# One address class for all tiles, and the conv's third input as seven quarter products: a hybrid decoder layer on one core

## The chip, the cores and the metric

The kernel runs on one core of one Trainium2 chip. The metric is the device time of one execution in microseconds: 962.82 us is the median of three runs of the kernel before (962.68 to 963.84). One more execution was profiled; it took 963.13 us, of which 961.4 us lie between its first and its last instruction (the span).

## What is computed

One decoder layer over 512 positions of 1,024 channels, in float32. Cut to its products and to what lies between them:

```python
h = rmsnorm(x, norm_mix_g)
proj = h @ w_in                      # 1024 x (9 * 1024 + 16)
bg, cg, xv, q, k, v, z, a, b, ga, gb = split(proj)
y_a = (bg * causal_dwconv(cg * xv, conv_a_w)) @ w_a_out      # 3 taps
y_b = gdn_branch(q, k, v, z, a, b, ...) @ w_b_out            # gated delta rule, chunks
mix = sigmoid(ga) * y_a + sigmoid(gb) * y_b
x = x + mix @ w_o
h = rmsnorm(x, norm_ffn_g)
up = causal_dwconv(h @ w_up, ffn_conv_w)                     # 1024 x 5632, 3 taps
x = x + (silu(up[gate]) * up[val]) @ w_down                  # 2816 x 1024
out = rmsnorm(x, norm_final_g)
```

`bg`, `cg` and `xv` are the three inputs of the short conv; `xv` is "the conv's third input" of the change.

## The kernel before, in words

**Products.** Each float32 matrix is held as the sum of a rounded part and a rest (`wh` and `wl` for weights, `x_[0]` and `x_[1]` for activations), and each product is made of three TensorE products: high by low, low by high, high by high. All go through `mm` (line 108), so the profile puts nearly all of TensorE's work on that one line.

**Jobs.** The kernel is a list of jobs that `run_jobs` takes in order. A job is a block of weights (1,024 x 256, 1 MB) and a use of it. While TensorE uses block i, ScalarE and VectorE split block i+1 into `wh` and `wl` tiles of 128 x 512 (`Block.part`, lines 137 to 141: a copy on ScalarE, then a subtraction on VectorE), and SP's queue loads block i+2. `wh` and `wl` have twelve slots each (`WQ`), so the split runs ahead of TensorE until it lacks a free slot. Small steps of work on the results (`evacs`), of the splits and of the delta rule's chain are put in between by `tick`, once for 2,048 columns of product.

**Two ways to use a block.** `col_job` makes two outputs of 128 x 512, each from 8 slices of the contraction with three products: 48 products of 512 columns in a job. A block is then split into 4 pairs of tiles. `sum_job` does the same 2 x 2 block product with 7 products of quarters in place of 8: its 7 weight tiles are sums and differences of the block's quarters (`SumBlock.split`, four extra VectorE operations at line 161), its activations are either quarters of the input or the sums held in `ts` (`us` in the second half), and its results are put together on VectorE and ScalarE (lines 292 to 309). It takes 84 products of 256 columns: 12 for each of 7 forms, in the order "11", "22", "s2", "s1", "s3", "s4", "12". "22", "s2", "s1" and "s3" take `ts`; the other three, 36 products, take the input itself.

**Where which is used.** The conv's groups 0 to 3 have three jobs each, `cg`, `xv`, `bg`. Group 0 is three `col_job`s. In groups 1 to 3 `cg` and `bg` are `sum_job`s; `xv` is a `col_job` in groups 1 and 2 and a `sum_job` in group 3 (lines 1141 to 1144). Then come three `sum_job`s and one `col_job` for `ga`, four `col_job`s each with `yas` and `yb` (`w_a_out`, `w_b_out`), the product with `w_o`, the 22 blocks of `w_up` (8 of them `sum_job`s) and the product with `w_down`. The products with `w_o` and `w_down` have the activations (`mix`, `mixb`, `xs`) as the stationary operand and the weights as the moving one; everywhere else the weights are stationary.

**What feeds VectorE in the conv's groups.** For a conv group the result of `cg` is held, `xv_c` multiplies by it (line 1121) and runs the conv's three taps (one ScalarE and two VectorE operations for each of two outputs, lines 335 and 338), and `bg_c` multiplies again (line 1130). All of this, the splits and the sums run on VectorE in the order in which they were issued.

**Where tiles lie.** A tile's address in its partition follows from the sizes of the tiles ahead of it, each rounded up to 32 bytes. In bytes, as the program before has them:

| tiles | address | modulo 256 |
|---|---|---|
| `wh`, 12 slots; `wl`, 12 slots | 19,232 + 2,048 n; 43,808 + 2,048 n | 32 |
| `hT`, `yb` (with its two halves in `hT`'s place), `h2` (`h` in the profile) | 68,384; 84,768; 101,152 | 32 |
| `ts`, `mix` (two tiles of 16,640 bytes) | 134,624; 151,264 | 224 |
| `yas` (in the same place, 32 elements further) | 134,752; 151,392 | 96 |
| `us`, `xs` | 151,520; 167,904 | 224 |
| `mixb` | 167,904 | 224 |

Slices of these tiles start at multiples of 512 or 1,024 bytes, so every operand of a product has its tile's remainder. The tiles from `ts` down the table are laid from the top end of the memory, those above from the bottom. A slot is taken over in the order in which slots come free, which is roughly, but not exactly, one after the other.

Of the kernel before, what the change touches and what calls it, by code (L numbers as in the profile page):

```python
# [9 lines left out]
F32 = mybir.dt.float32  # L10
# [6 lines left out]
P = 128  # L17
# [43 lines left out]
def layer_kernel(ctx, tc, x, norm_mix_g, w_in, w_ab, conv_a_w, gdn_conv_w, gdn_A_log, gdn_dt_bias,  # L61
# [60 lines left out]
            mm(o, ah, bh, False, i == n - 1, free)  # L122


    class Block:
        def __init__(self, src, quarter=(4, P)):
            self.src, self.quarter = src, quarter
            self.raw, self.ready, self.lead, self.fed = None, False, 2, True
            self.wh, self.wl = {}, {}

        def load(self):
# [3 lines left out]
            nc.sync.dma_start(out=self.raw, in_=self.src())  # L135

        def part(self, name, src):
            wh = self.wh[name] = wp.tile([P, *self.quarter], F32R, tag="wh", bufs=WQ, name=nm("wh"))
            wl = self.wl[name] = wp.tile([P, *self.quarter], F32R, tag="wl", bufs=WQ, name=nm("wl"))
            act.copy(out=wh, in_=src)  # L140
            dve.tensor_tensor(out=wl, in0=src, in1=wh.bitcast(F32), op=ALU.subtract)  # L141

# [8 lines left out]


    class SumBlock(Block):
        def split(self):
            if self.ready:
                return
            self.ready = True
            r = [self.raw[:, q] for q in range(4)]

            def to(q, a, b, op):  # L160
                dve.tensor_tensor(out=r[q], in0=a, in1=b, op=op)  # L161

            self.part("11", r[0])
            yield
            self.part("22", r[2])
            yield
            to(2, r[3], r[2], ALU.add)
            to(3, r[0], r[3], ALU.subtract)
            yield
            to(0, r[2], r[0], ALU.subtract)  # L170
            self.part("s2", r[0])
            yield
            self.part("s1", r[2])
            yield
            self.part("s3", r[3])
            yield
            to(0, r[1], r[0], ALU.subtract)
            self.part("s4", r[0])
            yield
            self.part("12", r[1])  # L180
            yield
# [34 lines left out]
            use(block.wh, block.wl)  # L216


    gate = const.tile([1, 16], F32, name="gate")

    def feed(raw):
        el = raw[0:1, 1].rearrange("p k n -> p (k n)") if len(raw.shape) == 4 else raw[0:1, 1]
# [204 lines left out]
    with tc.tile_pool(name="st1", bufs=1) as st1:  # L427
# [83 lines left out]
                                     op0=ALU.mult, op1=ALU.subtract)  # L511

        def round_k(q):
            wh = k_block.wh[q] = wp.tile([P, 4, P], F32R, tag="wh", bufs=WQ, name=nm("wh"))
            act.copy(out=wh, in_=k_block.raw[:, q])

        def rest_k(q):
            wl = k_block.wl[q] = wp.tile([P, 4, P], F32R, tag="wl", bufs=WQ, name=nm("wl"))
            dve.tensor_tensor(out=wl, in0=k_block.raw[:, q], in1=k_block.wh[q].bitcast(F32), op=ALU.subtract)


# [87 lines left out]
    Dms = {}  # L609

    def gates_chain(o):
        abT = gd.tile([P, S], F32, tag="cv", bufs=3, name="abT")[0:32]
        act.copy(out=abT, in_=o[0:32, :])
        yield
        o2 = bank()
        for n in range(NT):
            pe.transpose(out=o2[:, n * 32:(n + 1) * 32], in_=abT[:, n * P:(n + 1) * P], identity=ident[:32, :32])
        ab4 = o2[:, 0:128].rearrange("p (n c) -> p c n", c=32)
        abv = gd.tile([P, 16, NT], F32, name="abv")
        dve.tensor_copy(out=abv, in_=ab4[:, 16:32])  # L620
        dve.tensor_tensor(out=abv, in0=abv, in1=ab4[:, 0:16], op=ALU.add)
        T = lambda n: gd.tile([P, 32], F32, tag=n, name=nm(n))
        u, t, z, q, g = T("u"), T("t"), T("z"), T("q"), T("g")
        dve.tensor_tensor(out=hn(u), in0=abv[:, 0:8, :], in1=dtb.unsqueeze(2).broadcast_to([P, H, NT]), op=ALU.add)
        tc.keep_in_program_order(act.activation(out=hn(beta), in_=abv[:, 8:16, :], func=AF.Exp, scale=-1.0))
        tc.keep_in_program_order(act.activation(out=alg, in_=alg, func=AF.Exp))
        dve.tensor_scalar(t, u, -1.0, None, op0=ALU.mult)
        dve.tensor_tensor(out=t, in0=t, in1=u, op=ALU.min)
        tc.keep_in_program_order(act.activation(out=t, in_=t, func=AF.Exp))
        yield  # L630
        pool.tensor_scalar(beta, beta, 1.0, None, op0=ALU.add)
        pool.tensor_scalar(z, t, 2.0, None, op0=ALU.add)
        yield
        dve.reciprocal(out=beta, in_=beta)
        dve.reciprocal(out=z, in_=z)
        dve.tensor_scalar(u, u, 0.0, None, op0=ALU.max)
        yield
        pool.tensor_tensor(out=t, in0=t, in1=z, op=ALU.mult)
        pool.tensor_tensor(out=z, in0=t, in1=t, op=ALU.mult)
        pool.tensor_scalar(q, z, 1.0 / 15.0, 1.0 / 13.0, op0=ALU.mult, op1=ALU.add)  # L640
        for c in (11, 9, 7, 5, 3, 1):
            pool.tensor_tensor(out=q, in0=q, in1=z, op=ALU.mult)
            pool.tensor_scalar(q, q, 1.0 / c, None, op0=ALU.add)
        pool.tensor_tensor(out=q, in0=q, in1=t, op=ALU.mult)
        pool.tensor_scalar(q, q, 2.0, None, op0=ALU.mult)
        pool.tensor_tensor(out=g, in0=q, in1=u, op=ALU.add)
        pool.tensor_tensor(out=hn(g), in0=hn(g), in1=alg.unsqueeze(2).broadcast_to([P, H, NT]), op=ALU.mult)
        pool.tensor_scalar(g, g, -1.0, None, op0=ALU.mult)
        for _ in range(Y_G):
            yield  # L650
        o3 = bank()
        pe.matmul(o3[:, 0:32], lhsT=triu, rhs=g, start=True, stop=True)
        pe.matmul(o3[:, 32:64], lhsT=ones, rhs=g, start=True, stop=True)
        G, Gl = T("G"), T("Gl")
        dve.tensor_copy(out=G, in_=o3[:, 0:32])
        dve.tensor_copy(out=Gl, in_=o3[:, 32:64])
        dve.tensor_scalar(negG, G, -1.0, None, op0=ALU.mult)
        dve.tensor_tensor(out=kdv, in0=Gl, in1=G, op=ALU.subtract)
        act.activation(out=kdv, in_=kdv, func=AF.Exp)
        act.activation(out=eGl, in_=Gl, func=AF.Exp)  # L660
        act.activation(out=eG, in_=G, func=AF.Exp)
        dve.tensor_scalar(neG, eG, -1.0, None, op0=ALU.mult)
        yield
        o4 = bank()
        pe.transpose(out=o4[0:32, 0:P], in_=G, identity=ident)
        GT = gd.tile([32, P], F32, name="GT")
        dve.tensor_copy(out=GT, in_=o4[0:32, 0:P])
        nc.sync.dma_start(out=gtd, in_=GT)
        prep(0)
# [288 lines left out]
    def pair_jobs(pr):  # L958
        st = {}

        def qkv(which, j, o):
            c = gd.tile([P, S], F32, tag="cv", bufs=3, name=nm("cv"))
            yield from conv(c, o, gdn_w(which * 8 + 2 * pr + j), 4)
            if which == 1 and j == 0:
                reach(pr - 2, 99)
# [110 lines left out]
    def open_conv():  # L1076
        drain(evacs)
        drain(chains)
        drain(mids)
        drain(backs)  # L1080
        p2.close()
        sc = st["sc"] = p3.enter_context(tc.tile_pool(name="sc", bufs=1, side="right"))
        st["ts"] = [place(i, "ts").rearrange("p (m a n) -> p m a n", m=4, a=4) for i in range(2)]
        st["ya"] = sc.tile([P, ND, S], F32, name="ya")
        room["pool"] = sc
        adds.extend((Task(o_w.form()), Task(down_w.form())))
        sums_of.append(Task(activation_sums(hT, st["ts"], sc.tile([P, ND, S], F32, tag="mixa", name="xf"))))


    def place(i, name, up=0):  # L1090
        return st["sc"].tile([P, ND * S + 64], F32R, tag=f"t{i}", name=f"{name}{i}")[:, up:up + ND * S]

    def open_mix():
        st["mixa"] = st["sc"].tile([P, ND, S], F32, tag="mixa", name="mixa")
# [40 lines left out]
    for g in range(4):  # L1135
# [3 lines left out]
                     col_job(w_in, C_BG + g, hT, bg_c(g))]  # L1139
        else:  # L1140
            jobs += [sum_job(w_in, C_CG + g, hT, hsums, nothing, cg_place(g)),
                     sum_job(w_in, C_XV + g, hT, hsums, xv_c(g), pair_out) if g == 3 else
                     col_job(w_in, C_XV + g, hT, xv_c(g)),
                     sum_job(w_in, C_BG + g, hT, hsums, bg_c(g), pair_out)]

    def ga_c(g):
# [13 lines left out]
        return c  # L1160

    def split_ya():
        st["yas"] = [place(i, "yas", 32).rearrange("p (k n) -> p k n", k=ND) for i in range(2)]
        for k in range(ND):
            split(st["yas"], k, st["ya"][:, k, :])
            yield
# [24 lines left out]
    def wb_c(g):  # L1191
        def c(j, o):
            m = 2 * g + j
            t, mix = tmp("t"), st["mixa"][:, m, :]
            dve.tensor_tensor(out=t, in0=o, in1=sgb[0][:, m, :], op=ALU.mult)
            dve.tensor_tensor(out=mix, in0=t, in1=mix, op=ALU.add)
            yield
            if j == 1 and g % 2 == 1:
                if g == 1:
                    st["mix"] = [place(i, "mix").rearrange("p (m a n) -> p m a n", m=4, a=4) for i in range(2)]  # L1200
                yield from prep_a(mix_pairs(g - 1), st["mix"], g - 1)
        return c

# [248 lines left out]
    for g in range(NF // 2):  # L1452
# [6 lines left out]
        gj = up_job(g, gate_c(g), g < 2 or last, (lambda: splits.append(prep_d(prep_a, 0))) if last else None)  # L1459
        vj = up_job(NF // 2 + g, val_c(g), True)  # L1460
        gj[0].fed = vj[0].fed = g > 0
        jobs += [(gj[0], first_gate), (vj[0], first_val)] if g == 0 else [gj, vj]


# [216 lines left out]
```

## Time and profile before

| | us |
|---|---|
| median of three runs (lowest, highest) | 962.82 (962.68, 963.84) |
| profiled execution | 963.13 |
| its span | 961.4 |
| TensorE busy in the span | 950.7 (99%) |
| VectorE busy | 743.9 (77%) |
| ScalarE busy | 507.6 (53%) |
| GpSimd busy | 155.6 (16%) |

The granted TensorE clock is 0.998 of full speed. The page of the profile lists busy times by engine, the span in 40 slices, the chain that ended last, and groups of instructions. Products overlap in the records (each lasts longer than the distance to the next), so the time that a product costs is read from a stretch of the timeline divided by the number of products that start in it, and not from the mean duration. The count beside a stretch includes the records that reach into it from its edges.

### The profile page before, as it was taken

To read this page: it belongs to the slowest core of one execution; us is meant where nothing else is said; L and a number is where in the kernel's file an instruction comes from. 1 tells how busy PE (TensorE), PEld (TensorE's weight loads), DVE (VectorE), ACT (ScalarE), POOL (GpSimd) and SP (SyncE) were. 2 spreads that over 40 slices of the span, in tenths; PEclk is the share of its full clock that TensorE was granted. 3 is DMA by queue.
4 is the path that set the end of the run, shared out by engine and by line. 5 is a ranking of instruction groups with operands and counts; after the bars stand their busy time and mean duration, and the time that the engine had idled before them with its cause. 6 is when DMAs were issued, how large, how long until landed. Compare 5 with 4: busy or idle time off the path is not lost.

```text
span 961.4 us, 16188 instructions
## 1 busy us (share of the span) xinstructions
PE 950.7 (99%) x6188; PEld 823.1 (86%) x6188; DVE 743.9 (77%) x1401; ACT 507.6 (53%) x1073; POOL 155.6 (16%) x251
## 2 busy tenths in 40 slices
PE   8999999999999999999999999999999999999997
PEld 7888887987878889999988888998889999888885
DVE  6878686896725958799873479999988888969775
ACT  7895556565444434344651235645645456556463
POOL 3430300202000212312222100232222210000000
PEclk9999999999999999999999999999999999999999
DMA  6544312223121456667788435584775673176232
GB/s 227 157 137 123 94 53 89 75 57 93 53 89 45 144 130 140 175 162 170 215 270 174 120 112 217 152 231 162 177 191 180 185 160 132 45 264 228 100 132 88
DMA packets 51629, 138.11 MB, mean 144 GB/s; under 512 B 21691, under 2 KB 22112, under 8 KB 42848
## 3 DMA queue, kind: packets, MB, share of 16 engines
q1 hardware_dynamic: 38864, 107.45, 32.7%
q0 software_dynamic: 12544, 29.37, 16.1%
q8 instruction: 48, 0.79, 0.3%
q14 instruction: 29, 0.24, 0.1%
q10 hardware_dynamic: 144, 0.26, 0.1%
HBM read 133.64 MB, written 32.78 MB: 173 GB/s over the span
## 4 chain that ended last, share of the span: by engine, by line
PE 91%; DVE 4%; ACT 1%; issue 1%; POOL 1%; POOLq 0%
PE ps L108 83%; PE ps L689 1%; PE ps L724 1%; DVE wl L141 1%; PE ps L898 1%; PE ps L918 1%; DVE hn L1325 1%; DVE h L1339 1%; PE ps L907 1%; PE ps L886 0%; PE ps L885 0%; PE ps L862 0%; PE ps L856 0%; POOL r L1323 0%; PE ps L800 0%
## 5 line engine op out<-in xcount | busy, mean ns | idle before, releaser
L108 PE MATMUL ps<-hT,wh 128*128 128x512 f32 (+1 forms) x1104 | 318.1, 368 | 0.3 <-DVE hT L509 0.3
L140 ACT CAST wh<-raw 128x512 fp32r<-128x512 f32 x350 | 203.6, 619 | 217.0 <-PE ps L108 143.5
L141 DVE TENSOR_TENSOR wl<-raw,wh 128x512 fp32r<-128x512 f32 x350 | 233.3, 692 | 61.2 <-ACT wh L140 60.3
L108 PEld LDWEIGHTS ps<-hT,wh 128*128 128x128 f32 x1104 | 196.6, 189 | 28.9 <-DVE hT L509 0.5
L108 PE MATMUL ps<-hT,wl 128*128 128x512 f32 (+1 forms) x552 | 195.0, 361 | 0.0
L108 PE MATMUL ps<-h,wh 128*128 128x512 f32 (+1 forms) x704 | 177.7, 341 | 0.3 <-DVE h L1339 0.3
L108 PEld LDWEIGHTS ps<-h,wh 128*128 128x128 f32 x704 | 122.3, 189 | 15.6 <-DVE h L1339 0.5
L108 PEld LDWEIGHTS ps<-hT,wl 128*128 128x128 f32 x552 | 104.3, 189 | 13.8
L108 PE MATMUL ps<-h,wl 128*128 128x512 f32 (+1 forms) x352 | 114.5, 341 | 0.0
L108 PE MATMUL ps<-wh,xs 128*128 128x512 f32 (+1 forms) x320 | 96.9, 384 | 0.0
L108 PEld LDWEIGHTS ps<-h,wl 128*128 128x128 f32 x352 | 66.6, 189 | 7.6
L108 PEld LDWEIGHTS ps<-wh,xs 128*128 128x128 f32 x320 | 59.6, 188 | 13.1
L108 PE MATMUL ps<-wl,xs 128*128 128x512 f32 (+1 forms) x160 | 62.1, 388 | 0.0
L223 POOL COPY gate<-raw 1x1 f32<-1x1 f32 x38 | 16.7, 441 | 268.3 <-DMA raw<-in_w_in_dram 120.5
L338 DVE SCALAR_TENSOR_TENSOR cv<-ps,wA,cv 128x511 f32<-128x511 f32 (+2 forms) x72 | 53.2, 742 | 4.1 <-ACT cv L335 3.9
L108 PE MATMUL ps<-ts,wh 128*128 128x256 f32 x320 | 56.2, 276 | 0.0
L140 ACT CAST wh<-raws 128x512 fp32r<-128x512 f32 x66 | 39.3, 620 | 26.7 <-PE ps L108 8.9
L141 DVE TENSOR_TENSOR wl<-raws,wh 128x512 fp32r<-128x512 f32 x66 | 42.9, 687 | 12.5 <-ACT wh L140 12.5
L161 DVE TENSOR_TENSOR raw<-raw 128x512 f32<-128x512 f32 x72 | 49.5, 687 | 1.4
L108 PEld LDWEIGHTS ps<-ts,wh 128*128 128x128 f32 x320 | 49.0, 188 | 0.0
L108 PE MATMUL ps<-us,wh 128*128 128x256 f32 x256 | 45.0, 276 | 0.0
L108 PE MATMUL ps<-yas,wh 128*128 128x512 f32 x128 | 39.9, 391 | 0.0
(316 smaller groups left out, 1550.6 us busy)
## 6 DMA issues: line engine op xcount, KB each, us to landing
raw<-in_w_in_dram SPq DMA_DIRECT2D x35, 1024.0 KB, 5.3
raw<-in_w_up_dram SPq DMA_DIRECT2D x22, 1024.0 KB, 5.2
dv<-in_w_down_dram POOLq DMA_DIRECT2D x50, 256.0 KB, 6.1
raws<-dv SPq DMA_DIRECT2D x8, 768.0 KB, 5.8
ov<-in_w_o_dram POOLq DMA_DIRECT2D x20, 256.0 KB, 5.2
raws<-in_w_down_dram SPq DMA_DIRECT2D x10, 512.0 KB, 6.0
raw<-in_w_a_out_dram SPq DMA_DIRECT2D x4, 1024.0 KB
raw<-in_w_b_out_dram SPq DMA_DIRECT2D x4, 1024.0 KB, 6.6
```

The source lines that it names most:

```text
L108: pe.matmul(o, lhsT=a, rhs=b, start=start, stop=stop, skip_group_check=free)
L140: act.copy(out=wh, in_=src)
L141: dve.tensor_tensor(out=wl, in0=src, in1=wh.bitcast(F32), op=ALU.subtract)
L161: dve.tensor_tensor(out=r[q], in0=a, in1=b, op=op)
L223: tc.keep_in_program_order(pool.tensor_copy(out=gate[:, 0:1], in_=el[:, 0:1]))
L338: dve.scalar_tensor_tensor(out=dst[:, sh:], in0=src[:, :S - sh], scalar=wcol(j), in1=dst[:, sh:], op0=ALU.mult, op1=ALU.add)
L689: pe.transpose(out=o[:, n * P:(n + 1) * P], in_=src[:, n * P:(n + 1) * P], identity=ident)
L724: pe.matmul(o[:, i], lhsT=kqs[:, a, h, 0, sl], rhs=kqs[:, b, h, :, sl], start=a > 0, stop=a + b == 0)
L898: pe.matmul(o[:, 0:P], lhsT=TTf[:, f, :], rhs=rs[h], start=True, stop=True)
L907: pe.matmul(o2[:, 0:P], lhsT=kn[:, f, :], rhs=vns[h], start=True, stop=True)
L918: pe.matmul(o[:, 0:P], lhsT=A[:, f, :], rhs=vns[h], start=True, stop=True)
L1325: dve.scalar_tensor_tensor(out=hn_[:, sl], in0=x1[:, t, sl], scalar=r, in1=st["gff"][:, sl], op0=ALU.mult, op1=ALU.mult)
```

## The change

The diff has two parts.

*Layout.* `gate` grows from 16 to 64 elements (64 to 256 bytes). Each `wh` and `wl` slot grows from 512 to 528 elements, and a tile starts either at the slot's beginning or 16 elements (64 bytes) further: the blocks of `sum_job`, the first block (`k_block`) and the first two blocks of `w_up` start 64 bytes in, the others at the beginning. `place` goes: `ts`, `yas` and `mix` become plain tiles of 16,384 bytes, and `yas` is no longer moved by 128 bytes. To make room, the tiles `cv` have two buffers in place of three, and `wb_c` takes its temporary from the tag `c`, which `xv_c` used before, in place of a tag `t` of its own.

*Third input.* `xv` of groups 1 and 2 becomes a `sum_job`, as that of group 3 is.

```diff
+    UP = 16
+    def slot(tag, up, *dims):
+        t = wp.tile([P, 4 * P + UP], F32R, tag=tag, bufs=WQ, name=nm(tag))[:, up:up + 4 * P]
+        return t.rearrange("p (a b) -> p a b", a=dims[0]) if len(dims) == 2 else t
...
-            wh = self.wh[name] = wp.tile([P, *self.quarter], F32R, tag="wh", bufs=WQ, name=nm("wh"))
-            wl = self.wl[name] = wp.tile([P, *self.quarter], F32R, tag="wl", bufs=WQ, name=nm("wl"))
+            wh = self.wh[name] = slot("wh", self.up, *self.quarter)
+            wl = self.wl[name] = slot("wl", self.up, *self.quarter)
...
     class SumBlock(Block):
+        def __init__(self, src):
+            super().__init__(src)
+            self.up = UP
...
-    gate = const.tile([1, 16], F32, name="gate")
+    gate = const.tile([1, 64], F32, name="gate")
...
-            wh = k_block.wh[q] = wp.tile([P, 4, P], F32R, tag="wh", bufs=WQ, name=nm("wh"))
+            wh = k_block.wh[q] = slot("wh", UP, 4, P)
...
-        abT = gd.tile([P, S], F32, tag="cv", bufs=3, name="abT")[0:32]
+        abT = gd.tile([P, S], F32, tag="cv", bufs=2, name="abT")[0:32]
...
-            c = gd.tile([P, S], F32, tag="cv", bufs=3, name=nm("cv"))
+            c = gd.tile([P, S], F32, tag="cv", bufs=2, name=nm("cv"))
...
-        st["ts"] = [place(i, "ts").rearrange("p (m a n) -> p m a n", m=4, a=4) for i in range(2)]
+        st["ts"] = [sc.tile([P, 4, 4, HS], F32R, tag=f"t{i}", name=f"ts{i}") for i in range(2)]
...
-    def place(i, name, up=0):
-        return st["sc"].tile([P, ND * S + 64], F32R, tag=f"t{i}", name=f"{name}{i}")[:, up:up + ND * S]
...
-                     sum_job(w_in, C_XV + g, hT, hsums, xv_c(g), pair_out) if g == 3 else
-                     col_job(w_in, C_XV + g, hT, xv_c(g)),
+                     sum_job(w_in, C_XV + g, hT, hsums, xv_c(g), pair_out),
...
-        st["yas"] = [place(i, "yas", 32).rearrange("p (k n) -> p k n", k=ND) for i in range(2)]
+        st["yas"] = [st["sc"].tile([P, ND, S], F32R, tag=f"t{i}", name=f"yas{i}") for i in range(2)]
...
-            t, mix = tmp("t"), st["mixa"][:, m, :]
+            t, mix = tmp("c"), st["mixa"][:, m, :]
...
+        if g == 0:
+            gj[0].up = vj[0].up = UP
```

More of the change, by code (lines that the diff above doesn't have):

```diff
@@ L127, in __init__ @@
             self.src, self.quarter = src, quarter
-            self.raw, self.ready, self.lead, self.fed = None, False, 2, True
+            self.raw, self.ready, self.lead, self.fed, self.up = None, False, 2, True, 0
             self.wh, self.wl = {}, {}
@@ L513, in round_k @@
         def round_k(q):
-            wh = k_block.wh[q] = wp.tile([P, 4, P], F32R, tag="wh", bufs=WQ, name=nm("wh"))
+            wh = k_block.wh[q] = slot("wh", UP, 4, P)
             act.copy(out=wh, in_=k_block.raw[:, q])
         def rest_k(q):
-            wl = k_block.wl[q] = wp.tile([P, 4, P], F32R, tag="wl", bufs=WQ, name=nm("wl"))
+            wl = k_block.wl[q] = slot("wl", UP, 4, P)
             dve.tensor_tensor(out=wl, in0=k_block.raw[:, q], in1=k_block.wh[q].bitcast(F32), op=ALU.subtract)
@@ L1199, in c @@
                 if g == 1:
-                    st["mix"] = [place(i, "mix").rearrange("p (m a n) -> p m a n", m=4, a=4) for i in range(2)]
+                    st["mix"] = [st["sc"].tile([P, 4, 4, HS], F32R, tag=f"t{i}", name=f"mix{i}") for i in range(2)]
                 yield from prep_a(mix_pairs(g - 1), st["mix"], g - 1)
```

## The prediction

> **What bounds the kernel now.** I read the page first: its busy times, the granted clock and the chain of waits.
>
> ```profile
> span 961.4 us, 16188 instructions
> PE 950.7 (99%) x6188; PEld 823.1 (86%) x6188; DVE 743.9 (77%) x1401; ACT 507.6 (53%) x1073; POOL 155.6 (16%) x251
> PEclk9999999999999999999999999999999999999999
> PE 91%; DVE 4%; ACT 1%; issue 1%; POOL 1%; POOLq 0%
> ```
>
> TensorE has no idle time to win and its clock never drops. The kernel gets shorter only by fewer columns of product or by products that run closer together. So the second view is the groups by shape, for the counts (a row with `wl` and half the count belongs to each of these, and `mixb` adds 24 and 12):
>
> ```profile
> L108 PE MATMUL ps<-hT,wh 128*128 128x512 f32 x800 | 260.4, 400 | 0.0
> L108 PE MATMUL ps<-h,wh 128*128 128x512 f32 x384 | 119.8, 389 | 0.0
> L108 PE MATMUL ps<-wh,xs 128*128 128x512 f32 x304 | 94.0, 390 | 0.0
> L108 PE MATMUL ps<-h,wh 128*128 128x256 f32 x320 | 60.7, 284 | 0.3 <-DVE h L1339 0.3
> L108 PE MATMUL ps<-hT,wh 128*128 128x256 f32 x304 | 58.9, 284 | 0.3 <-DVE hT L509 0.3
> L108 PE MATMUL ps<-ts,wh 128*128 128x256 f32 x320 | 56.2, 276 | 0.0
> L108 PE MATMUL ps<-us,wh 128*128 128x256 f32 x256 | 45.0, 276 | 0.0
> L108 PE MATMUL ps<-yas,wh 128*128 128x512 f32 x128 | 39.9, 391 | 0.0
> L108 PE MATMUL ps<-yb,wh 128*128 128x512 f32 x128 | 39.6, 389 | 0.0
> L108 PE MATMUL ps<-wh,mix 128*128 128x512 f32 x88 | 27.8, 391 | 0.0
> ```
>
> The third view is stretches of the timeline, cut at the first product of each kind: 48 products with `ts`; 36 of 256 columns with `hT`; the `xv` job of group 1 (48 of 512), then its first 6 products alone; `yas` (192); `yb` (191); two `h` jobs (96); all with `xs` (456 of 512 columns, 24 of 256).
>
> ```profile
> core 0: us, PE busy (x), PEclk, DMA share, GB/s
> 386.43:391.89 5.46, 5.46 (x50) 1.00 0.99 269
> 382.13:386.43 4.30, 4.30 (x38) 1.00 0.81 271
> 364.33:375.24 10.91, 10.91 (x51) 1.00 0.77 168
> 364.33:365.72 1.39, 1.39 (x9) 1.00 0.76 93
> 484.88:528.84 43.96, 43.96 (x193) 1.00 0.81 210
> 528.84:572.18 43.34, 43.34 (x192) 1.00 0.40 116
> 638.10:659.89 21.79, 21.79 (x98) 1.00 0.49 122
> 846.70:954.00 107.30, 107.07 (x479) 1.00 0.48 166
> 951.50:954.15 2.65, 2.65 (x24) 1.00 0.11 41
> ```
>
> Divided, products of one shape differ with their tiles. 256 columns: 113.7 ns with `ts`, 119.4 with `hT`. 512 columns: 226.9 with `yb`, 227.0 with `h`, 229.0 with `yas`. The tail's 256-column products with `xs` stand about 117.8 apart (22.5 in 2.65 us), which leaves (107.30 - 24 x 0.118) / 456 = 229.1 for its 512-column ones. No engine is waited for in these stretches; what differs is where the tiles lie. With D for the stationary operand's remainder modulo 256 less the moving one's, the table of addresses gives: D = 0 (`hT`, `h`, `yb`) 119.4 and 226.9; D = 64 (`ts`, `us`) 113.7; D = 192 (`yas`, `xs`, `mix`) 117.8 and 229.0. No row shows D = 128, and none D = 64 at 512 columns.
>
> So most of the work already stands at the better end of what these rows show for 512 columns: 1,968 of 2,784 products at 226.9 to 227.3, 816 (`yas`, `xs`, `mix`, `mixb`) at 229. At 256 columns 864 stand at 113.7 and 936 at 119.4.
>
> The Trainium skill (SBUF — State Buffer, section "A bandwidth-pool intuition that's wrong (but worth ruling out)") gives TensorE two independent read ports, one for the moving operand and one for weight loads. By that rule D would not matter and the layout would be worth nothing; the 113.7 beside 119.4 ns for one shape speaks against it, but it stays a rival below.
>
> **Where the change puts tiles.** `gate` moves everything from the bottom by 192 bytes, and the 24 longer slots add 24 x 64 = 1,536, which is 6 x 256. So `hT`, `h2` and `yb` go from 32 to 224, the remainder that the tiles from the top have; `yas` goes from 96 to 224. All activations are then alike. The weights are not: a slot is 528 x 4 = 2,112 bytes, 8 x 256 + 64, and the first starts at 19,424, remainder 224. Slot n has remainder 224 + 64 n: the twelve slots go round 224, 32, 96, 160, three times. The 64 bytes of `up` turn this ring by one place and leave it a ring. A block's four or seven tiles take slots nearly in order, so each block meets all four D, and D changes from tile to tile; before, it was one value through a whole stage.
>
> **The sum, part by part.**
>
> *Third input.* Two jobs of 48 products (10.91 us) become jobs of 84: 48 at 113.7 and 36 at 119.4, which is 5.46 + 4.30 = 9.76. That is -1.15 each, **-2.3**.
>
> *256 columns.* Now (864 x 113.7 + 936 x 119.4) / 1,800 = 116.7 ns. Spread over four D: 119.4, 113.7, 117.8 and an unknown, for which I take their mean, so 117.0. On 1,800 products and the 168 new ones **+0.6**. Bounds: all at 113.7, -5.4 us; all at 119.4, +5.0.
>
> *512 columns.* 2,688 are left: 1,872 at about 227 and 816 at 229.0. With D = 0 for a quarter and the one row of unlike remainders (229.0) for the rest, the mean is 228.5: 1,872 x 1.5 = +2.8, 816 x -0.5 = -0.4. Then there is settling: the first 6 products of the `xv` job take 231 ns, 26 ns above pace together, before they fall into step. With a tile change every 2 to 6 products there are some 750 changes of D. I charge each a tenth of that settling, because only the address changes and not the length: +1.9. Together **+4.4**. Bounds: all at 226.9, -1.7; each product 5.7 ns above that, as D = 0 is above D = 64 at 256 columns, +13.6.
>
> *VectorE's new work.* Rows of before, for the stage of groups 1 and 2 and for group 3 with `ga`, then one sum job's operations:
>
> ```profile
> core 0: us, PE busy (x) PEld busy (x) DVE busy (x) ACT busy (x) POOL busy (x), PEclk, DMA share, GB/s
> 354.60:414.00 59.40, 59.40 (x422) 55.61 (x421) 48.67 (x81) 24.66 (x46) 12.72 (x20) 1.00 0.71 167
> 414.00:473.97 59.97, 59.97 (x518) 59.97 (x517) 52.67 (x91) 28.58 (x57) 12.49 (x22) 1.00 0.63 182
> ACT wh L140 <- PE ps L108: 15.6, 7, 4.3
> 413.82 0.68 DVE L297 TENSOR_TENSOR v<-ps,u 128x512 f32<-128x512 f32 x1
> 414.42 0.68 DVE L161 TENSOR_TENSOR raw<-raw 128x512 f32<-128x512 f32 x1
> 415.02 0.68 DVE L303 TENSOR_TENSOR o<-ps,v 128x512 f32<-128x512 f32 x1
> 415.62 0.41 DVE L305 TENSOR_TENSOR o<-ps,v 128x256 f32<-128x256 f32 x1
> 417.75 1.89 DVE L141 TENSOR_TENSOR wl<-raw,wh 128x512 fp32r<-128x512 f32 x3
> 466.90 2.49 DVE L141 TENSOR_TENSOR wl<-raw,wh 128x512 fp32r<-128x512 f32 x4
> ```
>
> Long operations follow each other 0.60 us apart, half ones 0.33. A sum job in place of a column job adds 3 `wl`, 4 of line 161, lines 297 and 303 and the halves of 293 and 305: 9 x 0.60 + 2 x 0.33 = 6.1 us, 12.1 for two, while TensorE's time for them shrinks by 2.3. So VectorE has 14.4 us less room. Cover: 10.7 idle in the first stretch, where ScalarE's copies wait 15.6 us for TensorE to free slots (this line of the waits belongs to that stretch alone), and the lead at the end: the last four `wl` are done from 467.5 on for a job that starts at 473.97, about 6.5. 17.2 covers 14.4 if at most 2.8 of it cannot be reached. In the second stretch VectorE left 7.3 idle though its lead was shrinking, so some idle time is a wait for ScalarE and stays. I take **+0.7**, with bounds 0 and 14.4 - 6.5 = 7.9 (none of the idle reached). Past that point `wl` of `bg` in group 3 and of the `ga` jobs is late, and TensorE waits for it. ScalarE gets 3 copies and 2 halves more for each job and is at 24.66 of 59.4; the blocks' loads and the POOL queue's DMAs for each job stay as they are.
>
> *Nothing:* `cv` with two buffers, because the third conv's first write and the Silu that empties its buffer stand in order on ScalarE (without that order, one conv's length, some 3 us, once); `c` for `t`, because no conv is left then.
>
> Sum: -2.3 + 0.6 + 4.4 + 0.7 = +3.4, on the profiled execution's 963.1 gives 966.5; the median lies 0.3 under that execution: **966.2**. Its own range is 963 to 971.
>
> **Rivals.**
> - *The slots' ring costs nothing.* The unlike D average out, or matter only over whole stages, and the third input alone counts: 962.8 - 2.3 = 960.5. For it: all observed differences are 1 to 5%. Against: 229.0 in 192 products in a row.
> - *The layout does what its words say,* every pair at the best row: 816 x -2.1 ns = -1.7, 936 x -5.7 = -5.3, and two jobs of 84 x 113.7 in place of 10.91 us = -2.7; with +1.5 for VectorE, about 954.6. Against it: the arithmetic of 2,112 bytes.
> - *VectorE becomes the bound* (slower side): its lead is used up in group 2, and from `xv` of group 3 to the last `ga` TensorE waits for `wl`. It decides when more than 2.8 us of the idle time can't be reached; at 6 us, with the layout as forecast, 971.5.
> - *D = 64 and D = 128 are bad at 512 columns,* 5.7 ns above: half of 2,688 x 5.7 = +7.7 in place of the 2.8 or so that they have in the sum: about 971 to 975.
>
> **How the numbers follow.** Forecast 0.45; the ring costs nothing 0.22; as its words say 0.10; VectorE 0.13; bad D 0.10. A difference under 0.2%, 1.9 us, can't be told from none here. Faster: 0.10 + 0.17 of the second = 0.27; the same: 0.05 of it and 0.10 of the forecast's lower end, 0.15; slower 0.58. The range 957 to 973 leaves out the layout as its words say and the upper part of the last two.
>
> **What would show it.** In the same stretches: `hT` and `yb` at 512 columns at 228 to 230 in place of 227, and no longer even from tile to tile; 256 columns near 117 for both kinds; the first six `sum_job`s of the conv at 9.8 us each; a wait of TensorE for `wl` of line 141 between 430 and 475 under 2 us. The forecast is wrong if 512-column products stand at 227 or less throughout, or if TensorE waits there for more than 3 us.

## The result, and the profile after

The changed kernel takes 974.12 us (median of 4 runs, 973.51 to 974.60) beside 963.33 us (962.68 to 964.52) for the kernel before on the same chip: ratio 1.011, 95% interval 1.0093 to 1.0128. The direction was forecast, the size was not: +10.8 us in place of +3.4, outside the range. The profiled execution took 973.51 us.

The page of the kernel after, its span, busy times, granted clock and the chain by engine:

```profile
span 971.8 us, 16362 instructions
PE 958.5 (99%) x6260; PEld 825.8 (85%) x6260; DVE 757.0 (78%) x1423; ACT 510.6 (53%) x1083; POOL 153.6 (16%) x251
PEclk9999999999999999999999999999999999999999
PE 81%; DVE 12%; ACT 2%; issue 2%; POOL 1%; POOLq 0%; ACTq 0%; DVEq 0%
```

The span grew by 10.4 us, the clock did not change, and TensorE is still busy for 99% of it: it is busy for 7.8 us longer. The chain shows something new too. VectorE's share of it went from 4% to 12%, at TensorE's cost.

Stretches of TensorE's timeline of the kernel after, each cut at the first product of its kind and of the next (length, TensorE busy with the number of records, granted clock, DMA share, GB/s). In order: 180 products of 512 columns with `hT`; 48 of 256 with `ts`; 36 of 256 with `hT`; `yas` (192); `yb` (192); two `h` jobs (96); then twice the 36 products of 256 columns with `hT` between two `ts` parts, later in the conv's groups:

```profile
315.41:357.12 41.71, 41.71 (x183) 1.00 0.43 124
358.49:364.09 5.60, 5.60 (x51) 1.00 0.40 88
364.09:368.36 4.27, 4.27 (x39) 1.00 0.38 159
489.10:533.59 44.49, 44.49 (x194) 1.00 0.88 233
533.59:578.03 44.44, 44.44 (x193) 1.00 0.39 113
643.77:666.00 22.23, 22.23 (x98) 1.00 0.49 121
413.15:418.21 5.06, 4.48 (x39) 1.00 0.38 43
443.37:449.38 6.01, 4.48 (x39) 1.00 0.75 222
```

At 512 columns that is 231.7, 231.7, 231.5 and 231.6 ns a product. The kernel before had 229.0 with `yas` and 226.9 to 227.2 with the others (the prediction shows its rows but for the same 180 products with `hT`):

```profile
313.68:354.58 40.90, 40.90 (x184) 1.00 0.43 125
```

All these stages now run at nearly one pace, and it is worse than the worst of before. At 256 columns the job shown has 116.7 with `ts` and 118.6 with `hT`, against 113.7 and 119.4. The last two rows have idle time inside a TensorE stretch, 0.6 and 1.5 us, which no such stretch had before.

Single products with `yb` of the kernel after (start, duration, line, operation, tiles):

```profile
545.14 0.40 PE L108 MATMUL ps<-yb,wh 128*128 128x512 f32 x1
545.38 0.39 PE L108 MATMUL ps<-yb,wl 128*128 128x512 f32 x1
545.61 0.39 PE L108 MATMUL ps<-yb,wh 128*128 128x512 f32 x1
545.83 0.39 PE L108 MATMUL ps<-yb,wl 128*128 128x512 f32 x1
546.07 0.39 PE L108 MATMUL ps<-yb,wh 128*128 128x512 f32 x1
546.29 0.40 PE L108 MATMUL ps<-yb,wl 128*128 128x512 f32 x1
546.53 0.40 PE L108 MATMUL ps<-yb,wh 128*128 128x512 f32 x1
```

In the kernel before, the products with `yb` stand evenly:

```profile
545.44 0.39 PE L108 MATMUL ps<-yb,wl 128*128 128x512 f32 x1
545.66 0.39 PE L108 MATMUL ps<-yb,wh 128*128 128x512 f32 x1
545.89 0.39 PE L108 MATMUL ps<-yb,wl 128*128 128x512 f32 x1
546.12 0.39 PE L108 MATMUL ps<-yb,wh 128*128 128x512 f32 x1
```

In the trace's nanoseconds these are 226 or 227 apart. In the kernel after, the distances from 545.14 on are 235, 229, 229, 231, 226, 236, 235. The stationary tile's slot changes at each of them, and D, worked out from the addresses that the program gives its tiles, goes 0, 128, 192, 64, 192, 64, 0.

VectorE in the conv's groups of the kernel after (busy time of PE, PEld, DVE, ACT and POOL), and what TensorE waited for (total, times, longest):

```profile
356.00:416.00 60.00, 59.42 (x504) 59.01 (x503) 54.43 (x92) 25.11 (x50) 12.58 (x20) 1.00 0.60 148
416.00:476.00 60.00, 58.47 (x500) 58.31 (x500) 56.74 (x98) 31.62 (x64) 12.93 (x22) 1.00 0.66 164
436.00:446.00 10.00, 9.88 (x86) 9.68 (x84) 9.97 (x17) 5.19 (x10) 2.85 (x4) 1.00 0.62 124
```

```profile
PE ps L108 <- DVE u L305: 2.3, 3, 1.5
```

TensorE is idle for 0.6 and 1.5 us in these two stretches of 60 us; in the like stretches of before it was busy throughout. Around a wait VectorE has nothing left: it is busy for 9.97 of the 10 us from 436 on.

Where the 10.4 us are, by stage, from the starts of the same products in both traces: 2.5 up to the first `ts` job, 1.7 in the conv's groups 1 to 3 and `ga`, 1.4 in `yas` and `yb`, 0.3 in the product with `w_o`, 4.5 from the first product with `h` to the end. By kind, summed over the distance from each product's start to the next (a distance over 1.2 times the usual pace of its kind counts at that pace, and the rest of it as a gap), for the two kernels and for two experiments told below:

| us | before | after | layout alone | third input alone |
|---|---|---|---|---|
| products of 512 columns: number, mean ns, sum | 2,784, 228.1, 635.1 | 2,688, 231.4, 622.0 | 2,784, 231.3, 644.0 | 2,688, 228.2, 613.3 |
| products of 256 columns | 1,951, 116.7, 227.8 | 2,119, 117.1, 248.2 | 1,951, 117.3, 228.9 | 2,119, 116.7, 247.3 |
| gaps | 13.7 | 17.0 | 13.9 | 19.3 |
| span | 961.4 | 971.8 | 972.4 | 964.7 |

So the change is, in products alone and at the paces of before, (2,119 - 1,951) x 116.7 ns - 96 x 228.1 ns = -2.3 us; the pace at 512 columns adds 622.0 - 613.3 = 8.7; that at 256 columns 0.9; the gaps 3.3. Together 10.6, against 10.4 of span. (The count at 256 columns includes the delta rule's own products, which the change doesn't touch.)

### The profile page after: what moved, and what is told of

It reads as the page before. It is cut to its first block, busy times and chain, and to the rows that moved or that the text cites. A ratio compares the mean times of both kernels' runs of the same rounds, so it can differ in the third digit from the quotient of the medians.

```text
span 971.8 us, 16362 instructions
## 1 busy us (share of the span) xinstructions
PE 958.5 (99%) x6260; PEld 825.8 (85%) x6260; DVE 757.0 (78%) x1423; ACT 510.6 (53%) x1083; POOL 153.6 (16%) x251
## 4 chain that ended last, share of the span: by engine, by line
PE 81%; DVE 12%; ACT 2%; issue 2%; POOL 1%; POOLq 0%; ACTq 0%; DVEq 0%
PE ps L108 74%; DVE wl L149 4%; DVE raw L173 2%; PE ps L701 1%; PE ps L736 1%; ACT wh L148 1%; DVE c L350 1%; PE ps L910 1%; PE ps L930 1%; DVE o L315 1%; DVE h L1346 0%; PE ps L919 0%; DVE hn L1332 0%; PE ps L898 0%; PE ps L897 0%
## 5 line engine op out<-in xcount | busy, mean ns | idle before, releaser
L108 PE MATMUL ps<-hT,wh 128*128 128x512 f32 (+1 forms) x1088 | 308.7, 364 | 2.6 <-DVE u L305 2.3
L149 DVE TENSOR_TENSOR wl<-raw,wh 128x512 fp32r<-128x512 f32 x356 | 236.3, 688 | 66.0 <-ACT wh L148 64.3
L108 PEld LDWEIGHTS ps<-hT,wh 128*128 128x128 f32 x1088 | 191.6, 188 | 31.2 <-issue 1.7
L108 PE MATMUL ps<-hT,wl 128*128 128x512 f32 (+1 forms) x544 | 188.8, 357 | 0.0
L108 PE MATMUL ps<-ts,wh 128*128 128x256 f32 x384 | 69.2, 279 | 0.0
L108 PEld LDWEIGHTS ps<-ts,wh 128*128 128x128 f32 x384 | 59.5, 189 | 0.0
L173 DVE TENSOR_TENSOR raw<-raw 128x512 f32<-128x512 f32 x80 | 54.9, 686 | 1.1
L108 PE MATMUL ps<-ts,wl 128*128 128x256 f32 x192 | 47.0, 279 | 0.0
```

What stands on the lines that cost most here:

```text
L108: pe.matmul(o, lhsT=a, rhs=b, start=start, stop=stop, skip_group_check=free)
```

## The experiments

Three theories stood at the start. Theory 1: D, the stationary tile's remainder modulo 256 less the moving one's, sets the distance of products, and the ring of 2,112-byte slots puts half of them at bad values and leaves them unsettled. Theory 2: the extra `sum_job`s make VectorE the bound, and that is the main loss. Theory 3: the alikeness of the tiles is itself bad, wherever they lie. Each kernel below computes the whole layer.

### The two parts alone

The layout without the third input:

```diff
-                     sum_job(w_in, C_XV + g, hT, hsums, xv_c(g), pair_out),
+                     sum_job(w_in, C_XV + g, hT, hsums, xv_c(g), pair_out) if g == 3 else
+                     col_job(w_in, C_XV + g, hT, xv_c(g)),
```

> The changed kernel's layout, with the conv's third input of groups 1 and 2 in 48 products of 512 columns as before. Theory 1 (the slots' ring): the loss lies in the distance of 512-column products, 231.7 ns on the mean in the changed kernel's trace in place of 227 and 229; on 2,784 products that is about +11 us, 256-column products stay near 117 on the mean, and TensorE does not wait for VectorE: 973 to 975 us. Theory 2 (VectorE's new work in the conv's groups is the loss): within 1.5 us of before, 962 to 964.5.

Measured: 973.99 us (973.48 to 974.27), ratio 1.0099, interval 1.0084 to 1.0114. The layout alone has nearly the whole loss: 10.0 of the 10.8 us.

The third input without the layout, the same lines the other way round in the kernel before:

> The kernel before with the third input of groups 1 and 2 as seven quarter products, its layout untouched. Theory 1: the products save 2.3 us and TensorE's waits for VectorE between 410 and 480 us give back about 3, as in the changed kernel's trace: 962 to 965 us. Theory 2: the whole loss, 970 us and more.

Measured: 965.71 us (965.21 to 966.50), ratio 1.0018, interval 1.0009 to 1.0028. What TensorE waited for in it:

```profile
PE ps L108 <- DVE u L293: 4.5, 4, 1.8
```

Its products are 2.3 us shorter, as worked out, and its gaps 5.6 us longer (19.3 against 13.7 in the table). Three of these four waits, 3.0 us, lie in the conv's groups. The fourth, 1.5 us, lies at 711 us and is no want of VectorE's time: from 705 to 710 VectorE is busy for 0.89 us, and ScalarE's copy of a block of `w_up` waits 4.78 us for its load.

```profile
705.00:710.00 5.00, 5.00 (x47) 5.00 (x46) 0.89 (x2) 1.41 (x3) 1.08 (x3) 1.00 0.65 247
708.45 1.14 ACT L140 CAST wh<-raw 128x512 fp32r<-128x512 f32 x2 [4.78 <-DMA raw<-in_w_up_dram]
```

So in this execution (966.37 us) VectorE's new work takes back somewhat more than the gain of 2.3 us. Theory 2 holds for a step of the sum and fails as the main cause. In the changed kernel the waits for `u` are 2.3 us in place of 3.0. There the products themselves are slower, which leaves VectorE more time. The kernel with D = 0 throughout, further down, has the third input too and 120.0 ns at 256 columns, and no wait for `u` stands among those of its TensorE; that the pace is the whole reason was not tried by itself.

### Slots of 2,304 bytes

In place of 2,112 bytes a slot gets 9 x 256, so that no ring arises: all 512-column products have D = 0, and nearly all of 256 columns D = 64. Twelve such slots do not fit, so there are eleven.

```diff
-WQ = 12
+WQ = 11
...
-        t = wp.tile([P, 4 * P + UP], F32R, tag=tag, bufs=WQ, name=nm(tag))[:, up:up + 4 * P]
+        t = wp.tile([P, 4 * P + 64], F32R, tag=tag, bufs=WQ, name=nm(tag))[:, up:up + 4 * P]
```

> The changed kernel with slots of 2,304 bytes (9 x 256) and eleven of them in place of twelve, so that every slot has remainder 224: D is 0 in all 512-column products and 64 in nearly all of 256 columns. Theory 1: 226.9 and 113.7 ns throughout; 1.7 and 5.3 us less than before in the old products, 2.7 less in the third input, and 1 to 4 us of waits for VectorE: 955 to 958 us. Theory 3 (it is the alikeness of the tiles from both ends that costs, not the ring): as slow as the changed kernel, 970 us and more.

> The same with the third input as seven products in group 3 alone: what the layout as its words say is worth by itself. Theory 1: 962.8 - 1.7 - 5.3 = 955.8 us, plus up to 1 us where a twelfth slot is missed. Theory 3: 970 us and more.

Measured: 966.83 us (965.10 to 969.50), ratio 1.0030, interval 1.0019 to 1.0040; and with `xv` as a `sum_job` in group 3 alone 967.33 us (966.68 to 967.79), ratio 1.0033, interval 1.0023 to 1.0043. Without the ring some 7 us of the loss are gone, which is Theory 1 again, and with all tiles alike the time isn't 970 or more, as Theory 3 would have it. At 512 columns these kernels run at 226.7 to 227.2. But 955 to 958 was expected, and two things were in the way. The first is at 256 columns. Whole jobs' `ts` parts with the 12 `hT` products ahead or behind left out, that is 48 products each, in the first of the two kernels, with a row of 36 `hT` products in between:

```profile
410.23:415.89 5.66, 5.66 (x51) 1.00 0.85 224
415.89:420.65 4.76, 4.41 (x38) 1.00 0.42 47
430.18:435.62 5.44, 5.44 (x51) 1.00 0.61 142
```

The same products with the same D = 64 take 117.9 ns in the first row and 113.3 in the last. From the first `ts` job to 415.9 all stand at 117.8. In the 36 products of the middle row TensorE waits for VectorE, and from then on they stand at 113.3 until the 512-column products of `ga`. In the `sum_job`s of the second half of the layer it is 117.8 again. The second kernel has no wait in the conv's stage and stays at 117.8 there and in the second half's `sum_job`s, also behind a wait of 1.4 us at 663. In both kernels most of the 256-column products of `w_up`'s first two blocks stand at 113.3 (48 in 5.44 us in the second kernel):

```profile
634.68:640.12 5.44, 5.44 (x50) 1.00 0.96 240
```

So D = 64 has two steady paces at 256 columns. The pace changed behind one wait and not behind another, so a wait alone does not decide. The second thing is a wait of TensorE for `kn` near 57 us from the start, 3.6 us in the first kernel and 2.7 in the second, followed up further down.

### One D through a whole stage

The kernel before with a pad of 192, 128 or 64 bytes ahead of `hT` and of the tiles of the second half, so that `hT`, `yb` and `h` lie at D = 64, 128 or 192 for the whole kernel (`cv` with two buffers makes the room). For 64:

```diff
+    hp.tile([P, 48], F32, name="hpad")
...
-            c = gd.tile([P, S], F32, tag="cv", bufs=3, name=nm("cv"))
+            c = gd.tile([P, S], F32, tag="cv", bufs=2, name=nm("cv"))
...
+        fp.tile([P, 48], F32, name="fpad")
```

(32 and 16 elements for the other two.)

> The kernel before (its cv tiles with two buffers) with 192 bytes left free ahead of hT and of x1, so that hT, yb and h2 have remainder 224 and all weights stay at 32: D = 64, without any ring, for the 1,968 products of 512 columns that had D = 0 and for the 936 of 256. Theory 1, with the value of unbroken stretches of D = 64 in the changed kernel's trace: 233 ns at 512 columns (+12), 113.7 at 256 (-5.3): about 970 us. If D alone does not matter and only its changing does: 227 ns and 963 or less.

> The same with 128 bytes left free: D = 128 for the same products. Theory 1: 230 to 233 ns at 512 columns (+6 to +12), 118 to 119 at 256 (-1): 968 to 974 us. If only the changing matters: 227 ns and 963.

> The same with 64 bytes left free: D = 192, which the kernel before has in yas, xs and mix. Theory 1: 229.0 ns at 512 columns (+4.1), 115 to 118 at 256 (-1.5 to -4): 963 to 966 us. If only the changing matters: 227 ns and 963 or less.

And the kernel after with slots of 2,048 bytes and no shift, so that every product in it has D = 0:

```diff
-        t = wp.tile([P, 4 * P + UP], F32R, tag=tag, bufs=WQ, name=nm(tag))[:, up:up + 4 * P]
+        t = wp.tile([P, 4 * P], F32R, tag=tag, bufs=WQ, name=nm(tag))
```

> The changed kernel with slots of 2,048 bytes and no tile shifted in its slot, so that every operand of a product has remainder 224 and D is 0 everywhere. Theory 1: 226.9 ns at 512 columns (-1.7 against before) and 119.4 to 120 at 256 for all (+4.9 in the sums ts and us), the two third inputs -1.7, and 1 to 3 us of waits for VectorE: 964 to 968 us. Theory 3: 970 us and more.

The stretch of `yb` (192 products of 512 columns) and one of 36 products of 256 columns (`hT`; for D = 0 the row is of `hT` too), D = 64, 128, 192 and 0 in this order:

```profile
532.09:576.88 44.79, 44.79 (x193) 1.00 0.38 112
386.87:390.95 4.08, 4.08 (x38) 1.00 0.91 288
```

```profile
533.75:578.37 44.62, 44.62 (x193) 1.00 0.39 112
386.80:391.07 4.27, 4.27 (x38) 1.00 0.79 251
```

```profile
530.03:573.98 43.95, 43.95 (x194) 1.00 0.39 114
383.76:388.00 4.24, 4.24 (x38) 1.00 0.85 258
```

```profile
530.53:574.05 43.52, 43.52 (x194) 1.00 0.43 119
361.73:366.05 4.32, 4.32 (x38) 1.00 0.33 138
```

| D | 512 columns, ns | 256 columns, ns | time of this kernel, us (one run each; before 963.84) |
|---|---|---|---|
| 0 | 226.7 | 120.0 | 966.14 |
| 64 | 233.3 | 113.3 | 968.77 |
| 128 | 232.4 | 118.6 | 971.96 |
| 192 | 228.9 | 117.8 | 966.01 |

The table is the missing part of the prediction. D = 64 is the best value at 256 columns and the worst at 512. That all D = 0 gives 966.14 and not 970 or more refutes Theory 3: it has the third input too, and its 256-column products run at 120.0.

The mean pace in the ring follows from the table to within 1.4 ns. In `yas` and in `yb` of the changed kernel each D has 48 of the 192 products; the mean of the four paces is 230.3, and measured are 231.7 and 231.5. The single products do not follow it. With each one's D from the program's addresses, the products of 512 columns stand at 230.8 (D = 0), 232.1 (64), 231.7 (128) and 231.6 ns (192) on the mean of the whole trace. Nor do the changes of D, 1,189 between neighbours, carry the excess: ahead of a product with another D the distance is 231.4, ahead of one with the same D 231.8. Between two products of D = 64 or of D = 128 the ring has 233.2 and 232.4, as in the table; between two of D = 0 or of D = 192 it has 230.2 and 230.9, 3.5 and 2.0 above the table. So the two good values do not come down to their own pace in the ring, where 999 of the 1,301 runs of one D are one or two products long.

### The price of the twelfth slot

```diff
-WQ = 12
+WQ = 11
```

in the kernel before, alone.

> The kernel before with eleven slots in place of twelve for `wh` and `wl`, nothing else. Theory: the three or so us that the kernels with slots of 2,304 bytes lost near 60 us from the start are the price of the missing twelfth slot: the split runs less far ahead, VectorE's steps of the delta rule come later, and TensorE waits 2.7 to 3.6 us for `kn` there; 966 to 967. Rival: they come from the address (D = 64), and with eleven slots alone the time is that of before, 963 to 964.5.

Measured: 967.18 us (966.72 to 969.03), ratio 1.0043, interval 1.0030 to 1.0057. What TensorE waits for in it that it did not wait for before:

```profile
PE ps L108 <- DVE kn L710: 2.6, 1, 2.6
```

The theory holds for the price and for where it arises: a step of the delta rule's chain, the second `kn`, starts on VectorE at 58.06 us in place of 52.98, and the same products start 3 to 4 us later from there on (the last 180 with `hT` ahead of the conv's groups at 316.90 in place of 313.68). How the missing slot delays that step was not followed further. The wait is not all of the price. Behind it the granted clock falls; of the three rows, two are of this kernel and one is of the kernel before:

```profile
58.00:61.00 3.00, 2.21 (x7) 0.80 0.03 5
61.00:64.00 3.00, 3.00 (x10) 0.63 0.00 0
61.00:64.00 3.00, 3.00 (x17) 1.00 0.51 153
```

Against the kernel before, the same 512-column products are 2.9 us later just behind the wait than ahead of it, and another 1.6 us later by 60 us. The kernels with slots of 2,304 bytes have the same wait, and the first of them has a clock of 0.53 from 61 to 64 us in its profiled execution; the second has 1.00. The ten executions of the first spread from 965.10 to 969.50, with mean clocks from 0.998 (the shortest) to 0.993.

### What sets the pace at D = 64

Slots of 2,304 bytes again, `xv` as a sum in group 3 only, and form "11" of each sum job unshifted (D = 0), so that in each job 12 products with D = 0 stand ahead of the 48 with D = 64:

```diff
         def __init__(self, src):
             super().__init__(src)
             self.up = UP
...
+            self.up = 0
...
+            self.up = UP
```

(around the part of form "11" in `SumBlock.split`). The second kernel of this pair has twelve slots for `wh`, eleven for `wl` and one buffer for `cv`.

> The kernel with slots of 2,304 bytes and `xv` as a sum only in group 3, but form "11" of each sum job lies at D = 0, the other six forms at D = 64, as in the kernel before the activations did (36 products with D = 0 ahead of 48 with D = 64). Theory: at 256 columns D = 64 has two paces, and which one holds depends on the products ahead: behind 256-column products with D = 0 it is 113.3 ns, behind 512-column ones 117.8. Then 72 of 84 products of a job stand at 113.3, some 1,700 x 4.5 ns = 7 us in part given back by 280 products at 120; about 962. Rival: 117.8 belongs to this layout whatever comes ahead; about 967.

> As the kernel with form "11" at D = 0, but with twelve slots for `wh` and eleven for `wl`, for which `cv` has one buffer. If the missing `wh` slot is what makes TensorE wait near 60 us, the wait is gone and the time about 3 us below that kernel's, 958.5 to 959.5 with the paces of the theory, faster than both kernels. If `wl` is what is short, or the pace of D = 64 stays at 117.8, it is within 1 us of the other kernel.

Measured: 968.05 us (967.05 to 968.74), ratio 1.0048, interval 1.0034 to 1.0062; and 967.89 us (967.58 to 970.20), ratio 1.0052, interval 1.0039 to 1.0064. Both miss. In the first, a `ts` part of 48 products, behind products with D = 0:

```profile
410.69:416.34 5.65, 5.65 (x51) 1.00 0.77 129
```

117.7 ns: products at D = 0 ahead do not bring the pace of 113.3. The remainders modulo 256 of both operands are those of the kernel before (32 and 224), and the pace isn't. What picks one of the two is open. It is not D modulo 512: in the kernel with slots of 2,304 bytes the products with 64 and with 320 stand at 117.8 together ahead of the wait at 416 and at 113.3 together behind it. Places modulo more than 512 weren't tried by themselves. In the second kernel the wait for `kn` is down to 0.2 us, but others stand at the same place:

```profile
PE ps L738 <- ACT kqs L991: 2.9, 1, 2.9
PE ps L108 <- ACT junk L768: 0.9, 1, 0.9
```

The granted clock is 0.65 and 0.50 in the two stretches of 3 us from 58 on. (The profiled execution is the longest of the five, 970.20 us.) So what the twelfth `wh` slot gave is taken again there. Whether the single buffer of `cv` or the missing `wl` slot takes it was not tried.

### The activations of the slow stages moved to D = 0

The one use of the table that needs almost no memory: in the kernel before, `yas`, `mix` and `xs` lie 64 bytes past the tile's start in place of 128 or none, so that they have the weights' remainder. The tiles that `us` and `xs` share grow by 256 bytes for it, which those of `ts` had already. `ts` and `us` stay at D = 64, and the 36 products with `mixb` stay at D = 192, so 780 of the 816 products move.

```diff
-        st["yas"] = [place(i, "yas", 32).rearrange("p (k n) -> p k n", k=ND) for i in range(2)]
+        st["yas"] = [place(i, "yas", 16).rearrange("p (k n) -> p k n", k=ND) for i in range(2)]
...
-                    st["mix"] = [place(i, "mix").rearrange("p (m a n) -> p m a n", m=4, a=4) for i in range(2)]
+                    st["mix"] = [place(i, "mix", 16).rearrange("p (m a n) -> p m a n", m=4, a=4) for i in range(2)]
...
-            st["xs"] = [st["up"].tile([P, 4, 4, HS], F32R, tag=f"t{e}", name=f"xs{e}") for e in range(2)]
+            st["xs"] = [st["up"].tile([P, ND * S + 64], F32R, tag=f"t{e}", name=f"xs{e}")[:, 16:16 + ND * S].rearrange("p (m a n) -> p m a n", m=4, a=4) for e in range(2)]
```

> The kernel before with `yas`, `mix` and `xs` moved to the weights' remainder (D = 0 in place of 192), `ts` and `us` left at D = 64; nothing else. Theory: 816 products of 512 columns go from 229.0 to 226.8 ns, -1.7 us, and the 24 of 256 columns hardly count: about 962.2, ratio 0.998. Rival (the distance is set by something else in these stages than D): the time of before, 963.8, within 0.1%.

Measured: 962.17 us (961.10 to 963.29, 11 runs) beside 963.24 us (962.85 to 964.58, 15 runs), ratio 0.9984, interval 0.9975 to 0.9993. The stretches of `yas` and `yb`:

```profile
484.93:528.45 43.52, 43.52 (x193) 1.00 0.81 212
528.45:571.98 43.53, 43.53 (x194) 1.00 0.40 115
```

Both now stand at 226.7; `yas` stood at 229.0. About 962.2 was forecast from the table, and this kernel is faster than both, by less than two tenths of a per cent.

## Why the prediction was right and wrong

*Right: what bounds the kernel, and the ring.* TensorE's pace decides, its clock does not move, and the arithmetic of 2,112 bytes gives a ring that puts about a quarter of the products at each D. The layout therefore costs time, and does not do what its words say.

*Wrong: the 512-column term,* forecast at +4.4, measured at +8.7. The step that failed is "the one row of unlike remainders (229.0) for the rest". D = 192 is 228.9, as that row has it, but D = 64 is 233.3 and D = 128 is 232.4. With the counts of the changed kernel at 512 columns, a mean of 230.4 in place of the forecast's 228.5, and of 227.6 before: 2.8 ns x 2,688 = 7.5 us where the prediction had 2.4 (+2.8 - 0.4). No row of the profile of before showed these two values, and the measured term lies between the stated bounds (-1.7 and +13.6); the value taken between the bounds lay too near the lower. *Settling* was forecast at +1.9, as a charge on each of some 750 changes of D. What is left for it is 8.7 - 7.5 = 1.2. There are more changes (1,189), but the excess isn't at them: it is in products of D = 0 and of D = 192 that do not reach their own pace. That this term came out small is no proof of its reason. What happened is the last rival, "D = 64 and D = 128 are bad at 512 columns", 5.7 ns above D = 0 by its price, 6.6 and 5.7 by the runs, and 971 to 975 us by its sum. It had a chance of 0.10. The trace held a hint for more: at 256 columns D = 64 and D = 0 differed by 5.7 ns, so 229.0 at one D said little about the two others.

*Right in the mean, in part by luck: the 256-column term.* +0.6 was forecast from a mean of 117.0 ns, and +0.9 was measured with 117.1. The parts of the mean are others: by the program's addresses D = 192 stands at 115.2 in the changed kernel, where the forecast had 117.8, and D = 128 at 118.2, where it had 117.0; D = 0 and D = 64 stand at 119.6 and 114.9.

*Right: the third input in products.* -2.3, and -2.3 by the counts. A job of 84 takes 368.36 - 358.49 = 9.87 us, forecast 9.8.

*Wrong in size: VectorE,* +0.7 forecast, +3.3 of gaps measured in the changed kernel (2.3 of them waits for `u`) and +5.6 in the third input alone (1.5 of them behind the late load at 711 us), within the bounds of 0 to 7.9. The cover of 17.2 us against 14.4 assumed that nearly all of VectorE's idle time could be reached. It couldn't: in the two stretches of 60 us in which TensorE comes to wait, VectorE still has 5.6 and 3.3 us idle in all, though hardly any around a wait. And what comes late is not `wl`, as the prediction named it. It is `u`, where VectorE adds a form's result to the copy of another (line 305) and reads the bank that TensorE writes next; the first such wait is at 414.7 us, earlier than the 430 that the prediction gave. So the rival "VectorE becomes the bound" was a real term of about half its price, added to the other.

*Right: nothing for `cv` and `c`.* The layout alone has gaps of 13.9 against 13.7 us, and no new wait of TensorE above 0.2 us, with two buffers of `cv`.

*The rule of the Trainium skill* (SBUF — State Buffer, section "A bandwidth-pool intuition that's wrong (but worth ruling out)") that weights and moving operands are read through two independent ports was set against one pair of rows in the prediction. The kernels with one D each decide against concluding from it that D does not matter: for one shape the pace goes from 226.7 to 233.3 ns with the addresses alone. Whether the two reads meet somewhere in the chip, and where, no run shows.

## What to carry to other kernels

A pace measured at one arrangement of operands bounds nothing about the arrangements that no row shows: where a layout brings new ones, price them by the whole spread seen anywhere, or measure each by itself first, as the kernels with one D did here. A slot size that isn't a multiple of the pattern's period turns a fixed offset into a ring of all offsets, so work out the address of the second slot and not only of the first. Idle time of an engine in a stretch is no cover until the profile shows that its work could have been issued there. And a wait has a second price where the clock falls behind it, so look at the granted clock in the stretch that follows.

## What the runs showed of the hardware

Where D stays the same through a stage, the distance of back-to-back products goes by D, and the order turns with the number of columns: D = 64 is best at 256 columns (113.3 ns against 120.0 at D = 0) and worst at 512 (233.3 against 226.7). That the difference counts at 512 columns, and not one operand's place, two values show with two pairs of remainders each: D = 0 with 32 and 32 (226.9, `yb` of the kernel before) and with 224 and 224 (226.7), D = 192 with 32 and 96 (229.0, `yas`) and with 224 and 32 (229.1, `xs`). D = 64 and D = 128 were held with one pair each.

At 256 columns D = 64 also has a second steady pace, 117.8 ns. In the kernel with slots of 2,304 bytes 117.8 turned into 113.3 behind one wait of TensorE for the next 60 us, in its sister kernel another wait changed nothing, and what decides is open. D = 192 has two as well: the last 24 products, with `xs`, stand 117.8 apart in the kernel before and 113.3 in the one with D = 64 for `hT`, `yb` and `h`, at the same remainders.

Behind a wait of 2.6 us near 56 us the granted clock fell to 0.63 for a stretch of 3 us in the kernel with eleven slots, and behind one of 3.6 us to 0.53 with slots of 2,304 bytes. Behind those of 2.7 us in the sister kernel and of 3.1 us in the one with form "11" at D = 0, and behind the one of 1.5 us at 446 us in the changed kernel, it stayed at 1.00.
